# Attention's last group in a hybrid decoder step: filler matmuls dealt 4-4-4-4-4-4-12-12 in place of 2-2-2-2-2-2-18-18

## The chip, the cores and the metric

The kernel runs on one core of a Trainium2 chip. The metric is the device time of one launch in microseconds; three runs of the kernel before took 2084.3, 2085.34 and 2087.26 us (median 2085.34 us). A core has a matmul engine (TensorE; PE for its matmuls, PEld for its weight loads), VectorE (DVE), ScalarE (ACT), GpSimd (POOL) and SyncE (SP), which here issues nearly all DMAs. Each engine works through its own queue in order and waits on semaphores that the others raise.

## The reference

One layer of a decoder trunk, for a prompt of 1024 tokens and eight sample tokens with carried state, width 1024, all in float32. Cut to what matters here:

```python
h  = rmsnorm(x) * (1 + scale1) + shift1
qkv, gdn_gate, beta_raw, a_raw, sq, sk, sv, ga, gb = split(h @ w_in)
q, k, v, beta, g = features(causal_conv4(qkv), beta_raw, a_raw)   # 8 heads of 128
o_a = gated_delta_rule(q, k, v, beta, g)                          # "delta stage"
y_a = (rmsnorm(o_a) * silu(gdn_gate)) @ w_gdn_out
o_b = sliding_window_attention(sq, sk, sv, sinks)                 # 16 query heads, 4 kv heads, window 128
y_b = o_b @ w_swa_out
x   = x + gate1 * ((sigmoid(ga) * y_a + sigmoid(gb) * y_b) @ w_o)
x   = x + gate2 * ffn(rmsnorm(x) * (1 + scale2) + shift2)
```

The projections to `ga` and `gb` are needed only after the delta stage, by the mix ahead of `w_o`.

## The kernel before

Activations lie transposed, features on the 128 partitions and tokens along the columns, in three parts of 384, 384 and 264 columns. Every large matmul is done in three passes over operands split into a high and a low half: `mm3` issues high by high (L180), low activations by high weights (L181) and high activations by low weights (L182). An output tile of 128 features is 3 parts x 8 contraction blocks, so 24 calls of `mm3`. A plain float32 matmul (transposes, the scan's products) leaves two records in the trace.

**Attention** runs four groups (one for each key/value head), each of eight blocks of 128 queries (`attention_group`, `attention_block`). A block does its scores in two halves into two score banks (`sc`, L614 and L615); ScalarE and VectorE copy them out under a mask (L618, L620); then come the maxima (L622 to L627), four exponentials with sums (L630), the denominator (L631, L632), the scaling (L635 on ScalarE, L637 on VectorE), four transposes (`pt`), the masking of the transposed block (`pc` L642, `pp` L646) and the products with the values (`pv`, L652). In the last group the matmuls of the sample attention (`qst`, `qa`, L704) lie among the first blocks.

**Filler** is work that nothing near needs. `gates` is a generator over the 16 tiles of `gb` and `ga`; one `next` on it, here called a step, issues one call of `mm3`: three matmuls of 384 columns (wide) or of 264 (narrow). At the end of a part ScalarE takes the tanh (L1294), POOL makes the sigmoid of it (L1295) and SP stores it (L1296); with each new tile SP loads weights (L135) that ScalarE and VectorE split (L129, L130). Behind the gates the same generator goes on with the output projection of the attention (`early_out`).

Filler is drawn in several places. In attention's last group, behind each block, a number of steps is drawn under `later(..., 120)`: recorded 120 priority places later than the code around it, and to be issued not before that block's score matmul (`issue_after(self.scored.ins)`). In the **delta stage** (`run`, the loop over eight heads) `pieces(n)` draws 8n steps: five times 8 in each of heads 0 to 5, more in heads 6 and 7. For each head `weave` lays several streams side by side: the inverse of a triangular block (`unit_inverse`, from L1019 to L1075), the scan over eight chunks (`delta_scan`: L947, L950, L954, L957, L958; 23 of its products carry the chain from chunk to chunk), the projections two heads ahead (`head_projections`, which starts with the output gate of the current head), the preparation of the next head (`delta_prepare`: transposes `tp`, L906, L907) and the filler.

Nothing in the code fixes the final order. Every instruction is recorded with a priority, and a scheduler places them engine by engine, by priority and by what its own model of the time says is ready; an engine then keeps the order that came out. So a number in one place can move instructions far behind it.

Of the kernel before, what the change touches and what calls it, by code (L numbers as in the profile page):

```python
# [64 lines left out]
class Step:  # L65
# [511 lines left out]
    def attention_group(self, pool, psum, g, Q, KH, KL, V, sink):  # L577

        nc = self.nc
        for n0 in (0, 4):  # L580
            ob = self.t(pool, [P, 2, 512], "obt", bufs=2)
            if 2 * g + n0 // 4 == 6:
                with self.tc.issue_after(self.x_load.ins):
                    self.later(self.sample_keys, 0)
                    self.later(lambda: self.sample_softmax(pool, psum), 0)
            for n in range(n0, n0 + 4):
                self.attention_block(pool, psum, g, n, Q, KH, KL, V, sink[:, 4 * g:4 * g + 4], ob)
                if g == 0 and n < 4:
                    for _ in range(3 if n == 3 else 2):
                        with self.tc.issue_after(self.scored.ins):  # L590
                            self.later(lambda: next(self.xrows), 50)
                if g == 3:
                    self.fill_psum = self.pmm
                    for _ in range(2 if n < 6 else 18):
                        with self.tc.issue_after(self.scored.ins):
                            self.later(lambda: next(self.filler), 120)
            for j in range(2):
                nc.sync.dma_start(self.ob[2 * g + j][:, n0 * P:(n0 + 4) * P], ob[:, j])
            for _ in range((2, 1, 1, 1, 2, 1, 0, 0)[2 * g + n0 // 4]):
                with self.tc.issue_after(self.x_load.ins):  # L600
                    self.later(lambda: next(self.mods), 100)
# [1470 lines left out]
```

## Time and profile before

| | before |
|---|---|
| runs, us | 2084.3, 2085.34, 2087.26 (median 2085.34) |
| span of the profiled execution, us | 2084.4 |
| mean granted clock of TensorE | 0.991 |
| HBM read and written, MB | 212.93 and 62.51 |
| last attention group, first scores to the end of its last idle gap | 340.4 to 376.6 us |
| delta stage, first scan product of head 0 to the last of head 7 | 499.9 to 1115.4 us |

The page gives the span of the profiled execution, from its first to its last instruction; the median of the runs is 0.9 us above it. In the views, a row of a stretch of time gives its bounds and length, then busy us (and number of instructions) on PE, PEld, DVE, ACT and POOL, the mean granted clock of TensorE as a share of full speed, the busy share of the DMA engines and GB/s. A row of the timeline gives start and duration in us, engine, line, operation, output and inputs, shapes and count; in square brackets stands how long the engine had idled before it, and on whom. A row of the waits gives total us, times, and the longest.

### The profile page before, as it was taken

Reading aid. Unit: us, or ns where it says so; the run is one execution under the profiler, and the core shown is the slowest. Engines: PE = TensorE matmul, PEld = TensorE weight load, DVE = VectorE, ACT = ScalarE, POOL = GpSimd, SP = SyncE. Lnnn points to the kernel's source line nnn. Section 1 sums busy time; section 2 is a strip of 40 time slices with the busy share of each in tenths; the row PEclk is TensorE's granted clock in tenths of the full one; section 3 lists DMA queues with packets and bytes.
Section 4 is the critical chain, followed back from the end, with each engine's and each line's share of the span. In section 5 each row is a group of like instructions: output and inputs, shape, how many; then the busy total and the mean of one; then the engine's idle time right before and its main releaser. Section 6 shows DMA issues by size and latency. Waiting matters only on the chain.

```text
span 2084.4 us, 41297 instructions
## 1 busy us (share of the span) xinstructions
PE 2012.7 (97%) x16245; PEld 1910.2 (92%) x16245; DVE 1347.8 (65%) x2714; ACT 900.2 (43%) x2233; POOL 520.2 (25%) x594
## 2 busy tenths in 40 slices
PE   7999998999999999989989999999999999999897
PEld 4987877799999999989989999999999999999897
DVE  5755768473655647656544675578876776767756
ACT  4664545433344243432342542354444444534443
POOL 2000000121321221201111000005575466446421
PEclk9999999999999999999999999999999999999999
DMA  8256443331332322312275855323333333488862
GB/s 300 62 144 210 135 167 116 117 94 51 80 80 61 73 72 52 89 42 62 63 223 172 285 186 163 112 63 97 105 91 112 102 92 112 136 305 266 291 215 94
DMA packets 301887, 275.75 MB, mean 132 GB/s; under 512 B 59730, under 2 KB 248111, under 8 KB 301676
## 3 DMA queue, kind: packets, MB, share of 16 engines
q1 hardware_dynamic: 295642, 252.14, 39.6%
q0 software_dynamic: 5552, 20.37, 2.8%
q8 instruction: 127, 2.08, 0.4%
q14 instruction: 68, 0.56, 0.1%
q10 hardware_dynamic: 498, 0.61, 0.1%
HBM read 212.93 MB, written 62.51 MB: 132 GB/s over the span
## 4 chain that ended last, share of the span: by engine, by line
PE 83%; DVE 5%; DMA 5%; ACT 3%; issue 1%; SPq 1%; POOL 1%; DVEq 0%; POOLq 0%; ACTq 0%
PE mm L180 19%; PE mm L181 18%; PE mm L182 18%; PE wv L180 3%; PE wv L182 3%; PE wv L181 3%; PE wy L182 2%; PE wy L180 2%; PE wy L181 2%; PE pv L652 1%; PE pt L190 1%; PE tp L190 1%; DVE x L1472 1%; PE mm L264 1%; PE rc L954 1%
## 5 line engine op out<-in xcount | busy, mean ns | idle before, releaser
L180 PE MATMUL mm<-b1h,wh 128*128 128x384 f32 (+1 forms) x1520 | 496.9, 328 | 3.7 <-ACT gt L1294 1.6
L181 PE MATMUL mm<-b1l,wh 128*128 128x384 f32 (+1 forms) x1520 | 489.3, 323 | 0.0
L182 PE MATMUL mm<-b1h,wl 128*128 128x384 f32 (+1 forms) x1520 | 488.0, 323 | 0.3 <-DVE wl L130 0.3
L180 PEld LDWEIGHTS mm<-b1h,wh 128*128 128x128 f32 x1520 | 286.7, 189 | 12.4 <-issue 4.6
L181 PEld LDWEIGHTS mm<-b1l,wh 128*128 128x128 f32 x1520 | 287.1, 189 | 4.4 <-issue 3.1
L182 PEld LDWEIGHTS mm<-b1h,wl 128*128 128x128 f32 x1520 | 286.3, 189 | 3.9 <-issue 2.8
L129 ACT ACTIVATE wh<-raw 128x1024 fp32r<-128x1024 f32 x83 | 87.0, 1049 | 122.4 <-PE mm L181 70.2
L130 DVE TENSOR_TENSOR wl<-raw,wh 128x1024 fp32r<-128x1024 f32 x82 | 101.0, 1233 | 57.2 <-ACT wh L129 55.1
L181 PE MATMUL mm<-pk,w 128*128 128x260 f32 (+1 forms) x440 | 124.8, 284 | 1.1 <-DVE pk L130 1.1
L180 PE MATMUL mm<-pk,w 128*128 128x260 f32 (+1 forms) x440 | 124.8, 284 | 0.0
L182 PE MATMUL mm<-pk,w 128*128 128x260 f32 (+1 forms) x440 | 124.5, 283 | 0.0
L130 DVE TENSOR_TENSOR w<-ws,w 128x512 fp32r<-128x512 f32 x88 | 78.0, 886 | 36.9 <-ACT w L129 36.7
L1626 ACT COPY bml<-mm 128x256 f32<-128x256 f32 (+1 forms) x132 | 48.9, 371 | 100.6 <-PE mm L182 96.7
L180 PE MATMUL mm<-bmh,w 128*128 128x260 f32 (+1 forms) x320 | 90.3, 282 | 0.0
L182 PE MATMUL mm<-bmh,w 128*128 128x260 f32 (+1 forms) x320 | 90.1, 282 | 0.0
L1681 DVE SCALAR_TENSOR_TENSOR fa<-fz,fcw,fa 128x512 f32<-128x512 f32 x88 | 75.2, 874 | 18.2 <-ACT fa L1679 17.9
L180 PE MATMUL mm<-b2h,wh 128*128 128x384 f32 (+1 forms) x256 | 83.2, 328 | 2.9 <-ACT wh L129 2.8
L181 PEld LDWEIGHTS mm<-pk,w 128*128 128x128 f32 x440 | 83.2, 189 | 1.3 <-DVE pk L130 1.3
L181 PE MATMUL mm<-b2l,wh 128*128 128x384 f32 (+1 forms) x256 | 83.6, 327 | 0.4 <-DVE b2l L130 0.4
L180 PEld LDWEIGHTS mm<-pk,w 128*128 128x128 f32 x440 | 83.2, 189 | 0.2 <-ACT bml L1626 0.2
L182 PEld LDWEIGHTS mm<-pk,w 128*128 128x128 f32 x440 | 83.4, 190 | 0.0
L182 PE MATMUL mm<-b2h,wl 128*128 128x384 f32 (+1 forms) x256 | 82.8, 326 | 0.0
(645 smaller groups left out, 5886.2 us busy)
## 6 DMA issues: line engine op xcount, KB each, us to landing
raw<-in_w_in_dram SPq DMA_DIRECT2D x59, 512.0 KB
ws<-in_w_ffn_down_dram SPq DMA_DIRECT2D x55, 256.0 KB
raw<-xd SPq DMA_DIRECT2D x47, 258.0 KB
raw<-in_w_ffn_down_dram SPq DMA_DIRECT2D x47, 256.0 KB
raw<-in_w_ffn_gate_dram SPq DMA_DIRECT2D x22, 512.0 KB
raw<-in_w_ffn_up_dram SPq DMA_DIRECT2D x22, 512.0 KB
qst<-in_w_mod_dram SPq DMA_DIRECT2D x16, 512.0 KB
raw<-in_w_mod_dram SPq DMA_DIRECT2D x16, 512.0 KB
```

Of the source, the lines that this page charges most:

```text
L129: self.nc.scalar.activation(hi, x, AF.Copy)
L130: (eng or self.nc.vector).tensor_tensor(lo, x, hi.bitcast(F32), op=ALU.subtract)
L180: mm(ps, whi, xhi, start=first, stop=False, **kw)
L181: mm(ps, whi, xlo, start=False, stop=False, **kw)
L182: self.last_mm = mm(ps, wlo, xhi, start=False, stop=last, **kw).ins
L190: self.nc.tensor.transpose(out, in_, self.ident[:p, :p])
L264: nc.tensor.matmul(ps[32 * j:32 * j + 32], self.cT[:, k0 + j, :], ws[j // 2][:, j % 2, :], start=k0 == 0, stop=k0 > 0)
L652: nc.tensor.matmul(pv[64 * r:64 * r + 64], V[:, n - back, ch], ps[:, r::2, :], start=back == 0, stop=back == (n > 0))
L954: yield step(nc.tensor.matmul(ds, kd[:, n, :], s, start=True, stop=True))
L1472: nc.vector.scalar_tensor_tensor(x[:, :np_], ps[:, :np_], by[:, j, 8:9], x[:, :np_], op0=ALU.mult, op1=ALU.add)
L1626: self.last_copy = nc.scalar.copy(r[p, i], x[p])
L1681: nc.vector.scalar_tensor_tensor(ai[:, c:e], zi[:, j + c:j + e], col(j), ai[:, c:e], op0=ALU.mult, op1=ALU.add)
```

## The change

One line. The number of filler steps behind the blocks of the last group:

```diff
                 if g == 3:
                     self.fill_psum = self.pmm
-                    for _ in range(2 if n < 6 else 18):
+                    for _ in range(4 if n < 6 else 12):
                         with self.tc.issue_after(self.scored.ins):
                             self.later(lambda: next(self.filler), 120)
```

The total is 48 steps either way (6 x 2 + 2 x 18, 6 x 4 + 2 x 12), so the filler drawn after the group, by the code, is the same.

Where the scheduler puts them, on PE, around the fifth block boundary of the group. Before, from the second score half of block 4 to the transposes of block 3 (`sc_4178` is that half, `mm_4218` filler, `sc_4226` the first half of block 5):

```order
L615 MATMUL sc_4178<-kl_2711,qst_3431 128x256
L180 MATMUL mm_4218<-b1h_12_150,wh_3990 128x384
L181 MATMUL mm_4218<-b1l_13_151,wh_3990 128x384
L182 MATMUL mm_4218<-b1h_12_150,wl_3991 128x384
...
L614 MATMUL sc_4226<-kh_2709,qst_3334 128x256
L615 MATMUL sc_4226<-kl_2711,qst_3334 128x256
...
L190 MATMUL pt_4142<-ident,E_4109 128x128 x4
L652 MATMUL pv_4151<-pc_4147,V_386 64x256 x2
```

The dots stand for one more step and for the scores of the second head of the pair. After the change, the same place one block on, from the second score half of block 5 to the transposes of block 4 (`mm_4247` is filler):

```order
L615 MATMUL sc_4268<-kl_2711,qst_3431 128x256
L180 MATMUL mm_4247<-b1h_14_152,wh_3990 128x264
L181 MATMUL mm_4247<-b1l_15_153,wh_3990 128x264
L182 MATMUL mm_4247<-b1h_14_152,wl_3991 128x264
...
L614 MATMUL sc_4325<-kh_2709,qst_3334 128x256
L615 MATMUL sc_4325<-kl_2711,qst_3334 128x256
...
L190 MATMUL pt_4232<-ident,E_4199 128x128 x4
L614 MATMUL sc_4332<-kh_2709,qst_3430 128x256
```

The first dots now stand for three more steps: four steps lie between a score half and the next, where two lay.

On ScalarE, in the first blocks of the group, the order changes too. One piece of the difference (`E_3945` is block 0, `E_4001` before and `E_4007` after are block 1; L630 are the exponentials, L635 the scaling):

```order
 L630 ACTIVATE E_3945,den_3966<-E_3945,m_3959 128x128 x4
-L618 ACTIVATE E_4055<-sc_4056 128x256
+L1294 ACTIVATE mrows_4067<-mm_3994 128x384
+L626 ACTIVATE es_4025<-es_4025 128x4
+L630 ACTIVATE E_4007,den_4029<-E_4007,m_4022 128x128 x4
+L618 ACTIVATE E_4071<-sc_4072 128x256
+L635 ACTIVATE E_3945<-E_3945,den_3966 128x128 x2
```

The exponentials of block 1 have moved in front of the scaling of block 0, with the tanh of a filler part.

Far behind, in the delta stage, on PE, at the end of head 3's scan (`rc_8741` is its last product on the chain, L1074 the end of the inverse for head 4, `rc_9632` the first scan product of head 4). Before, with `mm_10780` and `mm_10809` filler:

```order
L954 MATMUL rc_8741<-s_8739,kd_7856 128x128
L958 MATMUL o_8690<-s_8739,A_7908 128x128
L182 MATMUL mm_10780<-b1h_10_148,wl_10777 128x384
...
L1074 MATMUL tp_9175<-W_4535,UZ_8983 64x64 x8
L190 MATMUL tp_9874<-ident,K_8333 128x128 x4
L180 MATMUL mm_10809<-b1h_12_150,wh_10776 128x384
...
L190 MATMUL rc_8756<-ident,vn_7941 128x128 x4
...
L950 MATMUL rc_9632<-vn_8949,W_4535 128x128
L190 MATMUL tp_9885<-ident,K_8333 128x128 x4
```

The dots stand for 21, 14 and 2 more filler matmuls. After the change, the same place, nothing left out:

```order
L954 MATMUL rc_8741<-s_8739,kd_7856 128x128
L958 MATMUL o_8690<-s_8739,A_7908 128x128
L1074 MATMUL tp_9175<-W_4535,UZ_8983 64x64 x8
L190 MATMUL tp_9874<-ident,K_8333 128x128 x4
L190 MATMUL tp_9885<-ident,K_8333 128x128 x4
L190 MATMUL rc_8756<-ident,vn_7941 128x128 x4
L950 MATMUL rc_9632<-vn_8949,W_4535 128x128
```

No filler is left at this place; the rows are those that stand, before and after the change, at the end of head 4's scan. Counted over the whole order of PE, filler matmuls that stand from one head's first scan product to the next head's (wide and narrow):

| from the first scan product of | before | after |
|---|---|---|
| (all that stand ahead of head 0) | 362 (242, 120) | 364 (244, 120) |
| head 0 | 214 (142, 72) | 236 (164, 72) |
| head 1 | 113 (89, 24) | 192 (120, 72) |
| head 2 | 103 (55, 48) | 113 (89, 24) |
| head 3 | 113 (89, 24) | 31 (7, 24) |
| head 4 | 31 (7, 24) | 0 |
| head 5 | 72 (48, 24) | 72 (48, 24) |
| sum | 1008 | 1008 |

From head 6 on the counts are equal. The loads, splits and stores of the moved filler tiles move with it on SP, ScalarE, VectorE and POOL. In the second half of the kernel a group of four transposes of the convolution state (`wv_15387`) and some products of the second norm (L1496, L1506) stand up to some dozens of rows elsewhere.

## The prediction

> **What bounds the kernel now.** I read the busy shares first, then the chain that ended last.
>
> ```profile
> PE 2012.7 (97%) x16245; PEld 1910.2 (92%) x16245; DVE 1347.8 (65%) x2714; ACT 900.2 (43%) x2233; POOL 520.2 (25%) x594
> PE 83%; DVE 5%; DMA 5%; ACT 3%; issue 1%; SPq 1%; POOL 1%; DVEq 0%; POOLq 0%; ACTq 0%
> ```
>
> TensorE (PE) is busy for 97% of 2084.4 us and carries 83% of the chain. So time is won where PE idles and lost where PE is newly made to idle; moving a matmul from one busy place to another costs nothing. The change moves matmuls only, so two stretches matter: the one it aims at, and the one whose filler is taken. The first, by busy time in stretches (us, then busy of PE, PEld, DVE, ACT, POOL; granted clock, DMA share, GB/s):
>
> ```profile
> 342.00:354.00 12.00, 8.66 (x84) 6.77 (x84) 11.77 (x31) 7.35 (x26) 0.87 (x1) 1.00 0.35 120
> 354.00:366.00 12.00, 9.61 (x92) 6.79 (x90) 9.41 (x32) 7.09 (x29) 0.51 (x1) 1.00 0.11 31
> 366.00:378.00 12.00, 8.58 (x56) 5.85 (x55) 7.23 (x25) 7.44 (x31) 0.00 (x0) 1.00 0.12 47
> 378.00:402.00 24.00, 24.00 (x160) 21.53 (x160) 12.13 (x31) 12.70 (x45) 3.27 (x5) 1.00 0.17 53
> ```
>
> In the first six blocks of the last group PE idles 3.34 + 2.39 + 3.42 = 9.15 us; from 378 on, under eighteen steps a block, not at all. The waits of PE in that stretch, longest in total first:
>
> ```profile
> PE sc L614 <- DVE E L620: 4.2, 3, 2.3
> PE pv L652 <- DVE pc L642: 2.7, 4, 0.8
> ```
>
> Score products wait for VectorE (DVE) to empty a score bank, and the value products for the masked transposes. The second stretch is the delta stage, cut at the first scan product of each head (L950 `rc<-vn,W`), heads 0 to 5:
>
> ```profile
> 500.00:581.80 81.80, 80.99 (x740) 79.03 (x739) 45.55 (x101) 31.19 (x97) 21.59 (x25) 1.00 0.24 64
> 581.80:669.00 87.20, 86.50 (x764) 83.52 (x763) 52.53 (x112) 32.85 (x96) 15.79 (x24) 1.00 0.28 71
> 669.00:754.00 85.00, 84.37 (x760) 81.36 (x759) 51.06 (x110) 32.47 (x99) 17.22 (x23) 1.00 0.25 66
> 754.00:841.30 87.30, 86.60 (x764) 83.62 (x763) 52.59 (x112) 33.01 (x96) 15.80 (x24) 1.00 0.27 71
> 841.30:924.70 83.40, 76.96 (x688) 73.46 (x687) 51.05 (x110) 31.40 (x96) 14.57 (x21) 0.95 0.24 62
> 924.70:1010.30 85.60, 84.13 (x751) 80.97 (x750) 51.93 (x112) 32.70 (x99) 12.44 (x20) 0.99 0.24 63
> ```
>
> Heads 0 to 3 leave PE idle 0.6 to 0.8 us each. Head 4 leaves it idle 6.44 us, at a mean clock of 0.95: it is the head with little filler (31 filler matmuls against 103 to 113 in heads 1 to 3, by the table of the change).
>
> **Part one, attention.** Twelve steps move in front of block 6. A step is three matmuls, and their spacing is in the timeline of PE (start us, us):
>
> ```profile
> 372.59 0.34 PE L180 MATMUL mm<-b1h,wh 128*128 128x384 f32 x1
> 372.77 0.33 PE L181 MATMUL mm<-b1l,wh 128*128 128x384 f32 x1
> 372.94 0.34 PE L182 MATMUL mm<-b1h,wl 128*128 128x384 f32 x1
> ...
> 374.61 0.38 PE L614 MATMUL sc<-kh,qst 128*128 128x256 f32 x1 [0.81 <-DVE E L620]
> ...
> 375.19 0.60 PE L190 MATMUL pt<-ident,E 128*128 128x128 f32 x4
> 376.57 0.65 PE L652 MATMUL pv<-pc,V 128*64 128x256 f32 x4 [0.78 <-DVE pc L642]
> ...
> 845.58 0.28 PE L181 MATMUL mm<-b1l,wh 128*128 128x264 f32 x1
> 845.70 0.28 PE L182 MATMUL mm<-b1h,wl 128*128 128x264 f32 x1
> ```
>
> A matmul of 384 columns follows the one before after 0.173 us, one of 264 after 0.121: 0.52 and 0.36 us a step. By the order, steps 13 to 24 are four wide and eight narrow: 4 x 0.52 + 8 x 0.36 = 5.0 us. That much work could go into the 9.15 us of idle. What stands against it is the loop that sets the pace, on DVE:
>
> ```profile
> 373.85 0.16 DVE L631 TENSOR_TENSOR den<-den,es 128x4 f32<-128x4 f32 x1 [1.99 <-ACT E L630]
> 374.45 0.47 DVE L637 TENSOR_SCALAR E<-E,den 128x128 f32<-128x128 f32 x2
> 375.82 0.69 DVE L642 TENSOR_TENSOR pc<-pt,triu 128x512 f32<-128x512 f32 x1
> 377.43 0.16 DVE L627 TENSOR_SCALAR m<-m 128x4 f32<-128x4 f32 x1
> 379.31 0.16 DVE L631 TENSOR_TENSOR den<-den,es 128x4 f32<-128x4 f32 x1 [1.72 <-ACT E L630]
> ```
>
> The denominator releases the scaling, the scaled block the transposes on PE (375.19), these the masking, and behind the masking in DVE's queue stands the sign of the maxima (L627) that the next four exponentials wait for; they take until 379.31. That is 5.5 us a block, and PE's transposes are on it. The two steps of before ended at 374.61 - 0.81 = 373.80. Four end 1.04 us later, at 374.84, 0.23 us after the release at 374.61, so scores and transposes start some 0.2 us late. Over the five blocks behind the first that is 1.0 us. I take a gain of 5.0 - 1.0 = **4.0 us**. Bounds: 5.0 if nothing is late (9.15 if every wait went, for which I see no reason); at the other end the loop is 2 us longer than now, since ScalarE's order now has the four exponentials of block 1 in front of the scaling of block 0 (1.99 us by the row at 373.85). The last two blocks keep twelve steps, 12 x 0.52 = 6.2 us, more than the 5.5 us loop: no idle returns there.
>
> **Part two, the delta stage.** The number of steps up to the end of attention is unchanged, but the scheduler has re-sorted what follows, and the table of the change shows it: the filler matmuls by head go from 214, 113, 103, 113, 31, 72 to 236, 192, 113, 31, 0, 72. The filler that may be drawn before head 6 is fixed (the sums agree), so it now runs out one head earlier. PE's order in head 3, from its first scan product on, is now step for step that of head 4 before. What an uncovered end of a head looks like on PE, head 4 of before, and below it the covered end of head 3:
>
> ```profile
> 916.23 0.49 PE L950 MATMUL rc<-y,W 128*128 128x128 f32 x2 [0.75 <-DVE y L948]
> 917.48 0.49 PE L954 MATMUL rc<-s,kd 128*128 128x128 f32 x2 [0.77 <-ACT s L952]
> ...
> 919.81 1.97 PE L1074 MATMUL tp<-W,UZ 64*64 64x64 f32 x16 [1.61 <-ACT W L1065]
> 921.71 1.97 PE L190 MATMUL tp<-ident,K 128*128 128x128 f32 x8
> 923.81 1.11 PE L190 MATMUL rc<-ident,vn 128*128 128x128 f32 x4
> ```
>
> ```profile
> 836.30 1.14 PE L1074 MATMUL tp<-W,UZ 64*64 64x64 f32 x16
> 837.37 0.65 PE L190 MATMUL tp<-ident,K 128*128 128x128 f32 x4
> ```
>
> Two losses: the chain of scan and inverse is bare, and the clock falls: the same L1074 takes 1.97 us instead of 1.14, and the granted clock of this stretch is
>
> ```profile
> 915.00:925.00 10.00, 6.73 (x40) 5.61 (x39) 4.38 (x9) 8.03 (x30) 1.41 (x3) 0.70 0.03 8
> ```
>
> The price: head 3 holds 89 wide and 24 narrow filler matmuls (18.3 us), head 4 only 7 and 24 (4.1 us). With 14.2 us less work it lasts 83.4 us against 87.3, only 3.9 less: **10.3 us lost**. The parts agree: 6.44 - 0.70 = 5.7 us more idle, and 76.96 - (86.60 - 14.2) = 4.6 us more busy time for the same matmuls, the clock. Now head by head: head 0 +3.8 (22 wide), head 1 +11.2, head 2 +3.0, head 3 takes the old head 4's 83.4 (-3.9), head 4 loses its 4.1 us of filler, whose end is as bare as before (-4.1). Sum +10.0, and +0.3 for two matmuls more ahead of head 0. From head 5's first product to the end of the delta stage only small swaps are left, and in the second half some transposes and norms of a few us move; I cost these at nothing, because PE has matmuls to put around them, and at 1 us either way if not. Bounds of part two: 5.7 if only the idle returns; 10.3 + 4.1 = 14.4 if head 4 doesn't get shorter by the filler it loses, that is, if this stood in idle.
>
> Where DMAs move: the weight loads and the stores of the gates (SP's queue) go with their steps, and in one head a gate's store now stands on SP between the inverse's write and its read back (L1025, L1028), so a late gate would hold the inverse. A gate's part is 0.2 MB, and the DMA share in these heads is 0.24 to 0.28; I cost it at nothing.
>
> The sum: 2084.4 - 4.0 + 10.3 = 2090.7 us of span. The page gives only the span; the runs' median is 2085.34, 0.9 above it. Forecast **2091.6 us**, slower by 6.3 us or 0.3%.
>
> [...]
>
> **Rivals.**
> 1. *The moved filler isn't missed* (ends faster). If head 3's end found other ready matmuls, the 10.3 us would not come, and attention's 4.0 us would stand: 2081.3 us. It decides at a loss of 4.0 us in that end. For it: the filler is only shifted by one head and no matmul is added. Against it: that order on PE, which an engine can't leave. 0.09.
> 2. *The idle returns but not the clock.* Head 5's row, whose clock is 0.99 over the whole head, shows that gaps need not bring the clock down for long. Part two is then 5.7 us: 2085.3 - 4.0 + 5.7 = 2087.0 us. 0.19.
> 3. *Two bare heads in a row cost more than one.* Head 4 starts bare as well, with no filler behind its first scan products: its 4.1 us doesn't come off, and attention gives half: 2085.3 - 2.0 + 14.4 = 2097.7 us. For it: head 5, which started bare, lasted 85.6 us with 24 steps, where 37 steps made 87.3. Against: only 0.4 us of its idle is at its start. 0.17.
> 4. *The change does nothing in attention*: PE's in-order queue puts the steps on the loop and every block grows by what it takes in: 2085.3 + 10.3 = 2095.6 us. 0.10.
>
> The forecast itself has 0.45.
>
> **The numbers.** A measurement tells about 0.2% (4.2 us) of this kernel from no change: the borders are 2081.2 and 2089.5 us. Faster by more: half of the first rival, 0.05. Slower by more: rivals three and four, and most of the forecast's own case (down to 2089.5 if attention gives 5 and part two 9), 0.17 + 0.10 + 0.39 = 0.66. Within: 0.29. The range runs from 2084.5 (part two at 5.7, attention near its best) to 2098.0 (the third rival); outside lie the first rival and little of the ends.
>
> **What would show it.** In the changed profile the stretch of the first six blocks should leave PE idle 4 to 5 us in place of 9.15, and the last `pv` of the group should come some 4 us earlier. Heads 0 to 4, first scan product to first scan product, should last 85.6, 98.4, 88.0, 83.4 and 79.3 us; head 3 should show PE idle of about 6.4 us and a clock near 0.95, with L1074 at its end at 1.1 to 2.0 us behind a wait for ScalarE. The prediction is wrong if head 3 shows under 2 us of idle, or if the heads are as forecast and attention gains over 6 us. A clock of 1.00 in head 3 with 6 us of idle is the second rival; a head 4 over 82 us is the third.

## The result, and the profile after

| | before | after |
|---|---|---|
| median of 20 runs each, us (lowest to highest) | 2085.03 (2079.26 to 2093.31) | 2091.22 (2087.43 to 2099.16) |
| ratio after / before | | 1.0035, 95% interval 1.0027 to 1.0043 |
| span of the first profiled execution, us | 2084.4 | 2097.4 |

The change makes the kernel slower: by 0.35% in the ratio, which sets runs on one chip against each other, and by 6.2 us (0.30%) between the medians of all runs. The first profiled execution of the changed kernel happens to be the slowest of its twenty (2099.16 us), so two more profiles of each kernel were taken later (the runs "r" and "r2" below), and sizes are read from all three.

The page of after, busy shares first, then the chain of work that ended last:

```profile
PE 2019.3 (96%) x16245; PEld 1913.6 (91%) x16245; DVE 1350.3 (64%) x2714; ACT 900.6 (43%) x2233; POOL 510.7 (24%) x594
...
PE 55%; DMA 8%; DVE 8%; ACT 3%; issue 2%; SPq 2%; POOL 1%; DVEq 0%; POOLq 0%; ACTq 0%
```

The chain seems to have left PE (55% for 83%). The same row of the third profile of the very same program:

```profile
PE 79%; DVE 7%; DMA 7%; ACT 3%; issue 2%; SPq 1%; POOL 1%; ACTq 0%; DVEq 0%; POOLq 0%
```

So the shares of the chain swing by some twenty points from one execution to the next, and no cause is read from them here. The busy row is steadier: the same 16245 matmuls are busy 6.6 us longer (the mean granted clock is 0.987, where it was 0.991), and PE idles 78.1 us in place of 71.7.

**Attention.** Busy time in stretches of after (us, then PE, PEld, DVE, ACT, POOL, clock, DMA share, GB/s). The first score of the last group comes 2.3 us later than in the first profile of before, by a scatter ahead of it (339.3 to 342.7 us in the six profiles), so the stretches of the prediction are shifted by 2.3 us:

```profile
344.30:356.30 12.00, 10.16 (x91) 8.29 (x89) 11.63 (x28) 7.50 (x27) 1.38 (x2) 1.00 0.37 129
356.30:368.30 12.00, 10.62 (x84) 9.03 (x84) 8.28 (x28) 6.47 (x28) 0.00 (x0) 0.86 0.06 21
368.30:380.30 12.00, 10.39 (x75) 7.65 (x75) 7.28 (x25) 7.70 (x29) 0.51 (x1) 1.00 0.20 62
380.30:404.30 24.00, 22.86 (x147) 18.95 (x146) 14.40 (x38) 12.44 (x48) 4.77 (x8) 1.00 0.21 62
408.50:503.70 95.20, 93.58 (x799) 91.21 (x796) 54.15 (x98) 35.54 (x93) 15.97 (x25) 1.00 0.39 108
```

Four things stand here. Idle in the first three rows fell from 9.15 to 4.8 us, but the fourth, which was full, now has 1.1 of its own: the six blocks still idle 6.0 us. The second row's clock is 0.86, where it was 1.00. And behind the group (last row, up to the delta stage) there are 1.6 us of idle where there were none. The waits of PE in the first six blocks, longest in total first, and then behind the group:

```profile
PE pt L190 <- ACT E L635: 2.7, 2, 2.3
PE pv L652 <- DVE pc L642: 1.4, 3, 0.9
PE sc L614 <- DVE E L620: 1.1, 2, 0.7
```

```profile
PE mm L182 <- DVE wl L130: 1.6, 1, 1.6
```

The waits for VectorE shrank (4.2 to 1.1 and 2.7 to 1.4). At the top stands a new one: 2.3 us of the transposes for the scaling on ScalarE (L635), once. ScalarE's timeline at that place:

```profile
354.68 0.47 ACT L1294 ACTIVATE mrows<-mm 128x384 f32<-128x384 f32 x1
355.05 0.19 ACT L626 ACTIVATE es<-es 128x4 f32<-128x4 f32 x1
355.14 0.39 ACT L630 ACTIVATE E<-E,m 128x128 f32<-128x128 f32 x1
...
356.68 0.36 ACT L618 ACTIVATE E<-sc 128x256 f32<-128x256 f32 x1
356.94 0.68 ACT L635 ACTIVATE E<-E,den 128x128 f32<-128x128 f32 x2
```

The tanh of a filler part, the next block's four exponentials and a copy of scores stand ahead of the scaling that PE waits for: the piece of ScalarE's order that the change section shows. The denominator was ready 1.7 us before ScalarE came to the scaling, and VectorE began its own half (L637) at 355.30:

```profile
355.04 0.17 DVE L632 RECIPROCAL den<-den 128x4 f32<-128x4 f32 x1
```

**The delta stage**, from one head's first scan product to the next head's, heads 0 to 5:

```profile
503.70:589.50 85.80, 85.24 (x758) 82.24 (x758) 45.93 (x102) 32.73 (x103) 21.08 (x26) 1.00 0.26 69
589.50:688.20 98.70, 97.49 (x846) 95.18 (x845) 52.96 (x110) 33.85 (x96) 16.73 (x27) 1.00 0.26 69
688.20:775.50 87.30, 86.60 (x763) 83.63 (x762) 52.59 (x112) 32.93 (x96) 15.76 (x24) 1.00 0.27 71
775.50:856.20 80.70, 75.54 (x688) 72.10 (x688) 51.17 (x110) 31.49 (x96) 14.62 (x21) 0.96 0.24 64
856.20:932.30 76.10, 71.42 (x654) 67.50 (x653) 49.85 (x110) 29.89 (x96) 10.85 (x19) 0.97 0.22 57
932.30:1017.90 85.60, 84.33 (x751) 81.67 (x750) 51.36 (x111) 32.34 (x95) 12.46 (x20) 0.98 0.23 63
```

Head 3 has become the head without filler: 5.16 us of idle at a clock of 0.96 (0.70 at 1.00 before). Its end on PE (start, duration, wait and releaser in brackets):

```profile
847.75 0.49 PE L950 MATMUL rc<-y,W 128*128 128x128 f32 x2 [0.74 <-DVE y L948]
849.00 0.49 PE L954 MATMUL rc<-s,kd 128*128 128x128 f32 x2 [0.77 <-ACT s L952]
...
851.33 1.97 PE L1074 MATMUL tp<-W,UZ 64*64 64x64 f32 x16 [1.62 <-ACT W L1065]
853.23 1.97 PE L190 MATMUL tp<-ident,K 128*128 128x128 f32 x8
855.33 1.11 PE L190 MATMUL rc<-ident,vn 128*128 128x128 f32 x4
```

Wait for wait and at half clock (0.50 from 849.70 to 856.52), it is the end of head 4 of before. In the trace, PE's order over the whole of head 3 is that of head 4 before.

The whole, by landmarks of the timeline (first score of the last group, first and last scan products), in us; each cell has the first, second and third profile:

| stretch | before | after | mean difference | forecast |
|---|---|---|---|---|
| start to the first score of the group | 340.4, 342.4, 340.0 | 342.7, 339.3, 339.9 | -0.3 | 0 |
| first score to head 0 | 159.5, 159.7, 159.7 | 161.0, 162.8, 161.2 | +2.0 | -3.7 |
| heads 0 to 4 | 424.8, 424.3, 424.3 | 428.6, 429.0, 428.9 | +4.4 | +10.0 |
| head 5 to the last scan product | 190.6, 191.1, 190.2 | 191.6, 191.6, 192.1 | +1.1 | 0 |
| last scan product to the end | 969.1, 965.8, 965.7 | 973.5, 967.6, 966.5 | +2.3 | 0 |

The spans differ by 9.5 us on average in these three pairs, the medians of twenty runs by 6.2; the first pair, with the slowest of the changed kernel's twenty runs, carries most of that gap. From the first score to its last matmul, PE's idle is 48.0, 46.1 and 44.6 us before and 54.4, 51.6 and 49.5 after; the time at half clock is 35.6, 32.7, 35.2 and 46.3, 41.9, 39.9. Take the idle and half the half-clock time (an estimate, from the 0.50 granted in it) off the 1740 to 1755 us, and 1677 to 1679 us are left in all six. So to within 2 us the difference is idle and clock of PE.

### The profile page after: what moved, and what is told of

Its sections match the earlier page's. It is cut to its first block, busy times and chain, and to the rows that moved or that the text cites. A ratio compares the mean times of both kernels' runs of the same rounds, so it can differ in the third digit from the quotient of the medians.

```text
span 2097.4 us, 41303 instructions
## 1 busy us (share of the span) xinstructions
PE 2019.3 (96%) x16245; PEld 1913.6 (91%) x16245; DVE 1350.3 (64%) x2714; ACT 900.6 (43%) x2233; POOL 510.7 (24%) x594
## 4 chain that ended last, share of the span: by engine, by line
PE 55%; DMA 8%; DVE 8%; ACT 3%; issue 2%; SPq 2%; POOL 1%; DVEq 0%; POOLq 0%; ACTq 0%
PE mm L180 13%; PE mm L181 12%; PE mm L182 12%; PE wv L180 2%; PE wv L181 2%; PE wv L182 2%; DMA ws<-in_w_ffn_down_dram 1%; PE wy L180 1%; PE wy L182 1%; PE wy L181 1%; DVE pk L130 1%; DMA bmh<-in_w_ffn_down_dram 1%; DVE tmp L1019 1%; DMA raw<-in_w_ffn_down_dram 1%; DVE x L1472 1%
```

## The experiments

Three theories were on record for the first four runs. A, the prediction's: each uncovered end of a head costs 10 us, attention gains 4. B: the steps stand in the way of attention's loop. C: attention gives nothing.

### Five steps, and three steps

The same 48 steps, dealt otherwise. With five and nine the filler by head is that of before (214, 113, 103, 113, 31, 72), with three and fifteen that of after (236, 192, 113, 31, 0, 72):

```diff
-                    for _ in range(2 if n < 6 else 18):
+                    for _ in range(5 if n < 6 else 9):
```

```diff
-                    for _ in range(2 if n < 6 else 18):
+                    for _ in range(3 if n < 6 else 15):
```

> Five steps behind each of the first six blocks and nine behind the last two (48 in all). In this kernel the filler matmuls by head are those of before again: 362 ahead of head 0, then 214, 113, 103, 113, 31, 72. Theory A (the loss of the changed kernel is the second bare end of a head, 10 us, and attention by itself gains about 4): this kernel keeps attention's gain and has no second bare end, so 2081 us, 0.2% faster than before; head 3 idles PE under 1 us, head 4 about 6.4 us. Theory B (the loss comes from attention, where the steps stand in the way of the blocks): with more steps in the blocks it is slower than before, 2088 us or more, though the heads are as before. Theory C (attention gives nothing either way): 2085 us.

> Three steps behind each of the first six blocks and fifteen behind the last two (48 in all). Here the filler matmuls by head are those of the changed kernel: 364 ahead of head 0, then 236, 192, 113, 31, 0, 72. Theory A: the second bare end is there, attention gains only half: 2085 + 10 - 2 = 2093 us at most and not under 2089; heads 3 and 4 both idle PE by 4 to 6.5 us, and 80 to 84 us and 76 to 80 us long. Theory B: nearer to before than the changed kernel, 2085 to 2088 us, since fewer steps stand in the blocks. Theory C: as the changed kernel, 2091 us.

Measured: five and nine 2094.02 us, ratio 1.0037 (1.0025 to 1.0049); three and fifteen 2090.26 us, ratio 1.0019 (1.0010 to 1.0029). The kernel before ran at 2086.51 us beside them. Theory A's 2081 isn't there for the first. B's 2088 or more is, but not from the place that B named: attention's stretch is only 0.8 us longer than before. The second is in A's range (2089 to 2093) and near C's 2091. In the profile of five and nine, heads 0 to 4 last 423.3 us, as before. What is new stands in head 5:

```profile
925.00:1015.80 90.80, 85.59 (x750) 81.38 (x749) 52.77 (x112) 33.80 (x102) 14.31 (x20) 0.97 0.25 65
```

```profile
PE rc L190 <- DVE vn L976: 1.8, 1, 1.8
PE tp L1074 <- ACT W L1065: 1.1, 1, 1.1
```

Head 5 has the same 72 filler matmuls as before, but the scheduler has laid the head out otherwise: the ten gate matmuls that stood behind its last scan product now stand ahead of it, and the end is bare: 90.8 us for 85.5, with waits at its end as in head 4 and another of 1.0 us in the middle. So a bare end can turn up in another head, and that whole head, its middle wait included, is 5 us longer by it, not 10.

First score to head 0 is 160.5 us with five and nine. With three and fifteen it is 157.3, 2.3 below before:

```profile
340.20:497.50 157.30, 151.09 (x1227) 138.74 (x1226) 96.09 (x217) 71.53 (x222) 23.27 (x36) 1.00 0.33 94
```

PE idles 6.2 us there in place of 9.1, the wait for the scaling that four steps brought is missing, and no half clock falls. So attention can gain from more steps. Three and fifteen is still slower than before, since heads 0 to 4 take 429.7 us for 424.5 and the stretch from head 5 to the last scan product 2.8 us more.

### Holding the filler back

To cover the ends, each head's filler was held until the scan had got there: the first sixteen steps until the previous head's last scan product, the others until the head's own first. One run with two and eighteen, one with four and twelve:

```diff
-    def pieces(self, n):
+    def pieces(self, n, hold=None):
...
-            for _ in range(8):
-                next(self.filler, None)
+            with self.tc.issue_after(hold()) if hold and hold() else nullcontext():
+                [next(self.filler, None) for _ in range(8)]
...
-            if h + 2 >= H:
+            if self.scan.update({h: (self.scan.get(h, (ins.ins,))[0], ins.ins)}) or h + 2 >= H:
...
-                        streams[1:1] = [(chain(self.pieces(2), self.head_projections(pa, pool, h)), 100000, 100)]
-                        streams.append((self.pieces(3), 10000, 100))
+                        streams[1:1] = [(chain(self.pieces(2, lambda: h and self.scan[h - 1][1]), self.head_projections(pa, pool, h)), 100000, 100)]
+                        streams.append((self.pieces(3, lambda: self.scan[h][0]), 10000, 100))
```

> Attention as before (2 and 18), but in the delta stage each head's filler is held back: two pieces of eight steps until the scan of the head ahead has issued its last product, three until its own scan has issued its first. By the order the filler matmuls by head are 264 ahead of head 0 and then 120, 114, 123, 123, 114, 150: every end of a head has 40 or so filler matmuls. Theory A (bare ends cost): head 4's loss goes too, 2085 - 9 = 2076 us; heads 3 and 4 idle PE under 1.5 us each at full clock, head 4 lasts as long as head 3. Theories B and C (the ends don't matter): 2085 us, or slower if PE now idles ahead of head 0, where about 98 filler matmuls (17 us) are missing.

> The changed attention (4 and 12) with the filler of the delta stage held back head by head (264 matmuls ahead of head 0, then 120, 96, 141, 99, 120, 168). Against the kernel with 2 and 18 and the same holding this is attention's part alone. Theory A: 2072 us, 4 us under that kernel. Theory B: above it, by 4 us or more. Theory C: the same as it within 2 us.

Measured: 2095.96 us, ratio 1.0046 (1.0034 to 1.0058), and 2101.62 us, ratio 1.0061 (1.0046 to 1.0076). Heads 3 and 4 were cured (under 2 us of idle each, no half clock), but head 0 lost what it used to borrow. Its row in the first of the two:

```profile
498.80:578.90 80.10, 68.52 (x586) 62.90 (x585) 38.84 (x97) 25.98 (x84) 13.30 (x20) 0.83 0.23 60
```

11.6 us of idle and a clock of 0.83: the hole had moved, not closed. As a test of the price of an end the pair is lost. For attention it gave what theory B expected: four and twelve is 5.7 us above two and eighteen, and first score to head 0 lasts 164.9 us for 160.4, with 6.8 us at half clock where the other has none. But the intervals of the two overlap, and the filler by head isn't the same in both (114, 123, 123 against 96, 141, 99 in heads 1 to 3).

### Attention alone

Two pairs of numbers give the same total, and the same filler by head (204, 138, 144, 102, 0): two and sixteen, four and ten. Their difference was to be attention alone; but in the traces PE's order of heads 0, 4 and 5 isn't the same in the two, so attention is read on its own stretch below. Theory D is what was left of A: attention gives nothing, and the second bare end costs 4 to 5 us in all; its rival E has four steps cost time in attention itself. With them ran the first repeats of both kernels.

```diff
-                    for _ in range(2 if n < 6 else 18):
+                    for _ in range(2 if n < 6 else 16):
```

```diff
-                    for _ in range(2 if n < 6 else 18):
+                    for _ in range(4 if n < 6 else 10):
```

> Two steps behind each of the first six blocks as before, sixteen behind each of the last two: the attention of before with four steps less, which are drawn in the delta stage. Filler by head 204, 138, 144, 102, 0: head 4 bare as before, head 3 bare only behind its last four products. Theory A (of the prediction: a bare end costs 10): 2089 to 2092. Theory D (a bare end costs 4 to 5): 2086 to 2089. Its main use is as the base of the next run.

> Four steps behind each of the first six blocks, ten behind each of the last two: the same total as the run before, the same filler by head (204, 138, 144, 102, 0), so the difference of the two is attention alone. Theory A: 4 us below two and sixteen. Theory D: within 2 us of it. Rival E (the steps stand in the way of the blocks' loop or bring the clock down): 3 to 6 us above it.

Measured: 2096.90 us, ratio 1.0053 (1.0034 to 1.0071), and 2098.25 us, ratio 1.0056 (1.0038 to 1.0073). The intervals lie on each other, and the medians are 1.35 us apart with four steps the slower. First score to head 0, two and sixteen, then four and ten:

```profile
339.40:499.00 159.60, 148.88 (x1201) 135.94 (x1200) 93.77 (x213) 69.55 (x218) 25.12 (x35) 0.99 0.30 89
```

```profile
341.80:501.50 159.70, 150.04 (x1203) 136.50 (x1203) 97.01 (x214) 69.35 (x218) 25.01 (x35) 0.99 0.30 89
```

Both have one half-clock period of 3.41 us. With four steps PE idles 1.1 us less (10.7 to 9.7; in the blocks it falls from 9.2 to 6.0, behind them it rises from 1.6 to 3.7) and is busy 1.2 us more: 159.6 and 159.7 us. On this stretch theory A's 4 us of gain are not there, E's loss of 3 to 6 us neither, and D's bound of 2 us holds. That two and sixteen is so much slower than before was expected by no theory; its heads 0 to 4 last 431.3 us with 14 filler matmuls more (434.7 with four and ten), and the rest wasn't followed to single waits.

### The repeats

> The kernel before, unchanged, for a second profile: how far the lengths of stretches differ between two executions of one program. All theories: head 4 short of filler with 6 to 7 us of idle; the sums over attention's last group and over heads 0 to 4 within 1.5 us of the first profile.

> The kernel after, unchanged, for a second profile. Theory D (the bare end costs some 4 us in all, attention gives nothing): heads 0 to 4 sum to 427 to 430 us, first score to head 0 within 1 us of before, and the 5 us that its first profile lost behind head 6 are gone. Rival E (the four steps cost in attention itself): the stretch from the first score of the last group to head 0 is 1.5 us or more longer than before again, with half clock near the second block.

> The kernel before once more, for a third pair of profiles. If the half clock in attention falls by chance (fixed windows of 3.41 us, at another place of the program in each execution), first score to head 0 is 159.5 us, or 1 to 3 us more with as many half-clock windows; if it belongs to the order of the change, 159.5 again. Heads 0 to 4: 424 to 425 us.

> The kernel after once more. Heads 0 to 4: 428 to 429.5 us, so 4 to 5 over before and not 10; first score to head 0 161 to 163 us, so 1 to 3 over before and not 4 under it; from the end of the scan to the end 967 to 970 us if the 973 of its first profile was chance.

Their times were 2085.05, 2091.99, 2081.68 and 2090.29 us. They fill the second and third places of the table of landmarks: heads 0 to 4 repeat within 0.5 us, and the pairs differ there by 3.8, 4.7 and 4.6 us. First score to head 0 is never below before. The 973.5 behind the scan was in good part chance.

### The clock of the uncovered ends

Twelve matmuls on the identity, whose results the next product overwrites, were put into the waits of an uncovered end: two ahead of each of the last two scan products and eight ahead of the last products of the inverse. Up to the end of the delta stage nothing else in PE's order of before moved (in the second half some products did); in the order of after, a good part of head 4 and some of what follows did. Once in before (head 4), once in after (heads 3 and 4):

```diff
-            sp = self.t(psum, [P, P], "rc", bufs=2)
+            sp = warm(self, self.t(psum, [P, P], "rc", bufs=2), SP.get((h, n), 0))
...
-            ds = self.t(psum, [P, P], "rc", bufs=2)
+            ds = warm(self, self.t(psum, [P, P], "rc", bufs=2), DS.get((h, n), 0))
...
-        qp = self.t(psum, [64, NCH, 64], "tp", bufs=2)
+        qp = self.t(psum, [64, NCH, 64], "tp", bufs=2); warm(self, qp[:, 0, :], QP.get(h - 1, 0), self.scan.get(h - 1))
...
+SP, DS, QP = {(4, 7): 2}, {(4, 7): 2}, {4: 8}
...
+def warm(k, ps, n, after=None):
+    with k.tc.issue_after(after) if n and after else nullcontext():
+        for _ in range(n):
+            k.nc.tensor.matmul(ps, k.ident[:, :ps.shape[0]], k.ident[:, :ps.shape[1]], start=True, stop=True)
+    return ps
```

> The kernel before with twelve extra matmuls on the identity, whose results are overwritten, in the three waits at the uncovered end of head 4 (two ahead of each of the last two scan products, eight ahead of the last products of the inverse); all else stands in the order of before. Theory W (the clock is set by how much of a fixed window of about 3.4 us PE was idle, over about half of it halves the next): the 6.8 us at half clock at the end of head 4 go, the idle there falls from 3.1 to about 1, head 4 lasts 2.5 to 3.5 us less, the kernel 2082 to 2083. Rival L (the waits are latency of VectorE and ScalarE, and what runs at half clock there waits anyway): head 4 and the kernel within 0.7 us of before. Rival M (the extra matmuls stand in the scan's way): 1 to 3 us slower.

> The kernel after with the same twelve extra matmuls at the end of head 3 and again at that of head 4. Theory W: no half clock at either end, heads 3 and 4 together 5 to 7 us shorter than in the kernel after, which is what the second uncovered end cost in clock and more; the kernel 2085 to 2087. Rival L: within 1 us of after. Rival M: 2 to 6 us slower than after.

Measured: 2087.53 us, ratio 1.0000 (0.9987 to 1.0013), and 2090.87 us, ratio 1.0023 (1.0009 to 1.0037) against before, where after had 1.0035; the intervals of the last two overlap. In both profiles no half clock is left from head 0 to head 4 (8.9 to 9.1 us in before, 10.9 to 12.5 in after). Head 4 of before with them, then heads 3 and 4 of after:

```profile
846.10:928.00 81.90, 76.17 (x712) 71.98 (x712) 51.47 (x110) 31.50 (x98) 14.55 (x21) 1.00 0.24 63
```

```profile
773.10:853.10 80.00, 75.60 (x713) 72.09 (x712) 51.42 (x110) 31.87 (x98) 14.62 (x21) 1.00 0.25 65
853.10:927.40 74.30, 70.95 (x678) 67.87 (x677) 49.14 (x110) 29.61 (x92) 10.39 (x19) 1.00 0.22 58
```

81.9 us for 83.0 to 83.5, and 154.3 for 156.7 to 156.9 together: 1.3 us for each end where theory W said 2.5 to 3.5, and most of that isn't the end's. From the start of L1074 to the next head's first scan product it takes 4.9 us at all nine bare ends in the six profiles of before and after, and 4.5 at all three with the identity matmuls: 0.4 us an end. What else head 4 of before wins lies in its middle, where 3.4 us at half clock happen to be missing as well; what else head 4 of after wins lies ahead of its end, where its order changed. The half clock of an end also runs on into the next head (1.1 to 1.3 us in before, whose head 5 lasts 85.0 us for 85.5 with the identity matmuls). W was right that the half clock at the ends would go, and wrong on what that is worth; L, which expected no effect, was closer. The end of head 3 shows why:

```profile
848.60 1.14 PE L1074 MATMUL tp<-W,UZ 64*64 64x64 f32 x16 [0.54 <-ACT W L1065]
849.67 0.66 PE L190 MATMUL tp<-ident,K 128*128 128x128 f32 x4
850.77 0.66 PE L190 MATMUL tp<-ident,K 128*128 128x128 f32 x4 [0.45 <-ACT W L1075]
852.60 0.66 PE L190 MATMUL rc<-ident,vn 128*128 128x128 f32 x4 [1.17 <-DVE vn L976]
```

L1074 takes 1.14 us again, the transposes 0.66; what they save comes back as waits of 0.45 and 1.17 us for ScalarE and VectorE. At half clock, in after's rows at 853.23 and 855.33 above, no wait stands at these places: the transposes took 1.97 and 1.11 us, and the waits lay hidden under them.

## Why the prediction came out, and where it did not

**The time was right, and two of its terms were wrong.** 2091.6 us was forecast and 2091.2 measured, within the range, on the side that had the highest chance. But attention, forecast at -4.0, came at about +2, the heads at +4.4 in place of +10, and 1 to 3 us stand where the prediction had costed small swaps at nothing. So the agreement to 0.4 us is luck: by the table of landmarks the errors are +5.7 us from the first score to head 0, -5.6 in heads 0 to 4 and +3.1 elsewhere. The first two cancel, and the third is about what the profiled pairs differ by more than the medians of twenty runs (9.5 against 6.2 us). The sum hides this; the table of landmarks doesn't.

**Attention: the step that failed is "I take a gain of 5.0 - 1.0 = 4.0 us".** It counted what the steps could fill and one kind of delay. The three profiles give, against before: idle in the six blocks 9.15 to 6.0 (-3.2); new idle behind the group, 1.62, 1.88 and 0.43 (+1.3 on average), which in the first profile is PE waiting for a weight split of VectorE; half clock of 3.4, 6.8 and 6.8 us, half of it lost (+2.8, an estimate from the 0.50 granted in it); and about 1 us of matmuls that now stand ahead of head 0 (five more of 384 columns in the trace, 5 x 0.173 = 0.9). That makes +1.9, for 2.0 measured. The wait of 2.3 us for the scaling was in the prediction, as the far bound of this very term (ScalarE's order, the 1.99 us row), and was not taken. It costs twice: as idle, and as the clock behind it (0.50 from 358.18 to 361.60 in the first profile; the second period of the two profiles with 6.8 us stands 24 us further on, behind three waits of 0.4 to 0.7 us).

How much of the clock's part belongs to the change is less sure. Before had a wait as long of its own (2.35 us, for a score bank). Its order of the blocks was profiled six times (before three times, held two and eighteen, two and sixteen, before with identity matmuls): four lost no clock there, one 3.4 us and one 6.8. The order with four steps was profiled six times too (after three times, held four and twelve, four and ten, after with identity matmuls), and all six lost 3.4 or 6.8 us. By these averages, 1.7 and 5.7 us, the change costs, by the same estimate, some 2.0 us of clock rather than 2.8. The fourth rival, that attention gains nothing, was the one to come true here in its outcome, and the stretch of four and ten against two and sixteen shows it apart from the heads. With three steps, without the wait for the scaling, it did gain (2.3 us).

One sum of this part was wrong without harm: the last block's twelve steps aren't all wide but four wide and eight narrow, 5.0 us, less than the loop's 5.5; no wait of PE came of it.

**The heads: the mechanism was right, the term of 10.3 us was mis-sized.** Filler runs out one head earlier; head 3's end is that of head 4 before, with about the forecast idle. Heads 0, 1 and 2 came within 0.8 us of 85.6, 98.4 and 88.0. Heads 3 and 4 came at 80.7 and 76.1 for 83.4 and 79.3. The price had been taken from the whole of head 4 of before, as though all its loss stood at its end. A part stood in its middle:

```profile
889.00 0.74 PE L1038 MATMUL tp<-MR,U 32*32 32x32 f32 x64 [1.12 <-DVE MR L1034]
892.19 0.80 PE L950 MATMUL rc<-y,W 128*128 128x128 f32 x2 [1.55 <-DVE y L948]
```

```profile
888.30:891.71 3.41, 1.64 (x68) 1.31 (x68) 3.30 (x4) 0.37 (x1) 0.00 (x0) 1.00 0.51 149
891.71:895.12 3.41, 2.93 (x10) 2.93 (x11) 2.65 (x5) 1.41 (x3) 0.00 (x0) 0.50 0.00 0
```

Two waits of 2.7 us together, and 3.4 us at half clock behind them, half of it lost by the same estimate: 4.4 us (4.0 and 3.7 in the other profiles) that have to do with VectorE's queue at that place and not with the end. In head 3 of after one wait is left of it:

```profile
825.13 0.49 PE L950 MATMUL rc<-y,W 128*128 128x128 f32 x2 [1.40 <-DVE y L948]
```

That is 1.2 us of wait on average (1.40, 1.10, 1.18), with no half clock behind it, for 4.0, so head 3 is 2.8 us shorter than the head it was priced by; and head 4, which was to lose only its filler, lost this as well, but for 0 to 1.0 us: 3.5 us. Taken off the forecast of 10.0 that leaves 3.7, for 4.4 measured.

Since the order in the two heads is the same, the difference can be placed. Head 3 of after is 2.7 us shorter than head 4 of before on average, and all of it lies ahead of L1074: 1.3 us up to the end of the wait for `y`, and 1.4 from there to L1074 (27.6 us in the three profiles of before, 26.2 in those of after). Five and nine has that order in its head 4 once more, with both waits (0.95 and 1.55 us), and there the middle kept full clock: the mean of 0.97 over the head comes to 4 to 6 us at half clock (an estimate), about what the end takes in before (5.7), where the whole head 4 of before has 9.1 (0.95):

```profile
842.70:925.00 82.30, 75.83 (x688) 72.03 (x687) 51.37 (x110) 31.35 (x96) 14.59 (x21) 0.97 0.24 63
```

From the wait to L1074 it takes 26.2 us, as in after. So the 3.4 us at half clock cost 1.4 there, a little under the half counted above. No run took the waits themselves away, so their part, and that of head 4 of after, rests on the profiles.

The second term of the price, 4.6 us of "more busy time for the same matmuls, the clock", counted busy time as lost time. By the identity matmuls, giving the clock back wins only 0.4 us from L1074 to the end of the head, since PE then waits there for ScalarE and VectorE (0.45 and 1.17 us, above).

**The rivals.** The moved filler was missed: the first rival is out. The second had the wrong mechanism, since the clock did fall,

```profile
849.00:859.00 10.00, 7.77 (x48) 6.65 (x49) 4.21 (x9) 8.63 (x39) 1.40 (x3) 0.66 0.11 40
```

but its price, 5.7 us, was nearer to 4.4 than the forecast's. The third is out: head 4 took 76 us, not over 82. The sign named for it, and that for head 3's idle (about 6.4 us, 5.2, 5.4 and 4.9 seen), did their work. Of the two signs for attention, idle of 4 to 5 us came as named in the three rows (4.8 us) and misled, since the idle went on in the row behind; the other (the last `pv` 4 us earlier) said at once that this term was wrong: from the first score to the last `pv` it is 65.8 us where it was 63.7.

What stays open: the 1.1 us between head 5 and the end of the scan, where head 6 idles 2 us longer and head 7 takes part of it back, and whether the 2.3 us behind the scan are more than the scatter, which is 3.4 us among the profiles of before alone. No version here beat before; the nearest, before with the identity matmuls, is level with it.

## What to carry to other kernels

Price a stretch that returns elsewhere by the waits of that stretch, one by one, and not by the length of the whole loop turn that held it: what else went wrong in the same turn doesn't move along. Half-clock time on a chain that waits for other engines was mostly hidden here (0.4 us for nearly 5 at the end of a head), and where PE sets the pace it cost near half its length (1.4 for 3.4 in the middle of a head): price the two apart. And where a scheduler re-sorts, filling idle in one queue can be undone by the order of another: read the order of the engine that PE waits for as well. Here three steps won 2.3 us in attention, and four lost 2.0 behind a new wait for ScalarE.

## What the runs showed of the hardware

In the fourteen profiles nearly every period at half clock lasts 3.41 us or a multiple of it, and inside one execution their starts lie a whole number of 3.413 us apart, from the first blocks to the last (in the first profile of before they start at 891.71, 919.02 and 1089.69 us, for one: 8 and 50 times 3.413 apart). The row of windows around the new wait of attention, cut on that grid:

```profile
351.35:354.77 3.42, 3.42 (x47) 2.97 (x46) 3.34 (x11) 3.17 (x13) 0.00 (x0) 1.00 0.00 0
354.77:358.18 3.41, 1.14 (x10) 0.97 (x10) 2.37 (x14) 3.41 (x17) 0.51 (x1) 1.00 0.53 211
358.18:361.60 3.42, 3.42 (x13) 3.42 (x12) 2.15 (x8) 1.80 (x9) 0.00 (x0) 0.50 0.02 5
361.60:365.01 3.41, 3.21 (x46) 2.42 (x49) 2.56 (x9) 2.14 (x9) 0.00 (x0) 1.00 0.00 0
```

A window with PE busy for 1.14 of 3.41 us, and in the next the granted clock is 0.50. Counted over all windows of the fourteen profiles (behind the first 60 us and ahead of the last 12):

| idle of PE in a window, us | full clock: next stays full | next is half | half clock: next is full | next stays half |
|---|---|---|---|---|
| under 0.5 | 7694 | 0 | 98 | 14 |
| 0.5 to 1.0 | 180 | 0 | 2 | 18 |
| 1.0 to 1.5 | 133 | 7 | 0 | 10 |
| 1.5 to 1.9 | 15 | 22 | 0 | 4 |
| over 1.9 | 0 | 71 | 0 | 10 |

By these counts the clock fell behind none of the 7874 windows at full clock with under 1.0 us of idle and behind all 71 with over 1.9; it came back behind 98 of the 112 at half clock with under 0.5 and behind none of the 24 with over 1.0. The end of head 3 of after and the lone wait in its middle fit this: in the first profile the window with the first two waits of the end (0.74 and 0.77 us) idles 1.52 us, and the next is at half clock; the window with the lone wait of 1.40 us idles 1.40, and the next stays full. The grid lies elsewhere in the two first profiles: counted from the start of the span it stands at 0.83 us in before and at 3.19 in after. And the same order lost windows in one execution and none in others: attention kept full clock in all three profiles of before, and had 6.8 us at half clock in the run with identity matmuls, whose order there is the same; first score to head 0 lasted 162.4 us in it for 159.5 to 159.7.

Of the 100 falls counted here, 81 came with no gap of PE as long as a window, and in one of them the longest gap was only 0.69 us; so in these profiles a fall went with the idle summed over a window, by the table, and not with the longest gap alone. In the first profile of before, the end of head 4, whose longest gap is 1.61 us, ran at a clock of 0.70 (915 to 925 us), while the wait of 2.35 us in attention lies across two windows, 1.36 us of it in one and 0.99 in the next, and both were followed by full clock.
